# One transformer layer on one core: another written order for the MLP's up projection (transposes between products, early pairs begin with product 3) and two steps of the down projection split ahead

## The chip, the core and the metric

The kernel runs on one core of a Trainium2 chip. The core's engines have queues of their own and run at the same time: TensorE (PE: matmuls and transposes into PSUM banks, with PEld its weight loads), VectorE (DVE), ScalarE (ACT), GpSimd (POOL) and SyncE (SP, here a queue that issues DMAs). They wait for each other by semaphores. The metric is the device time of one execution in microseconds. The kernel before takes 1562.1 us (median of three runs, 1558.93 to 1566.71).

## What is computed

One layer of a hybrid encoder over 1024 tokens of width 1024 (plus 16 learned tokens): a combined input projection, neighbourhood attention, a gated linear recurrence in two directions, a gated mix with its output projection, and an MLP. The change lies in the MLP alone, the last third of the time:

```
D_MODEL = 1024
D_FF = 4 * D_MODEL
...
m = rms_norm(h, norm_mlp[l])
h = h + jnp.square(jax.nn.relu(m @ w_up[l])) @ w_down[l]
...
h = rms_norm(h, norm_final)
return h[:, N_META:]
```

All of it is float32. `m @ w_up` is a product of 1024 x 1024 with 1024 x 4096, and its squared positive part goes through `w_down` (4096 x 1024).

## The kernel before

**Float32 by three products.** A factor is split into a high half (`hi`, ACT casts it to `fp32r`) and a low half (`lo`, DVE subtracts the high half from the source). A product is then hi·hi + hi·lo + lo·hi. For a weight block `weights()` does this: ACT writes `wh` (L988), DVE writes `wl` (L989).

**Seven products for eight.** The 32 column blocks of `w_up` are taken as 16 *pairs* of 128-column blocks. For each pair the 2 x 2 block product is computed with seven block products instead of eight (a Winograd scheme). `pair_sums` makes the sums s1 to s4 of the weight blocks a11, a12, a21, a22 with four DVE operations (L682 to L685); the activations have sums of their own (t1 to t4). A block product is a `chain` of 12 matmuls of 128 x 512: four slices of the inner dimension, three matmuls each (L691, L692, L693). The seven are:

- product 1 (a11 x b11) and product 2 (a12 x b21, added on top) in a bank `pa`; ACT copies p1 out between the two (L1051), and the result is block u11.
- product 3 (s4 x b22) in a bank `pc`; ACT copies p3 out (L1061).
- product 6 (s2 x t2) in a bank `pb`; DVE makes u1 = pb + p1 (L1066).
- product 5 (s1 x t1) on top of `pc`; DVE adds pc to u1 (L1070), ACT applies relu and square.
- product 7 (s3 x t3) on top of `pb`; DVE makes u3 = pb + p1 (L1081), POOL subtracts p3 (L1082) and writes a block out (`block_out`, L1075).
- `finish_u3`: DVE adds pc (L1087), ACT relu and square, POOL two more blocks.
- product 4 (a22 x t4) on top of `pb`; DVE u2 = pb + p1 (L1096), ACT relu and square, POOL the last block.

Since a chain on top of a bank changes it, it has to wait until whoever read the bank's earlier content is done: product 7 waits for L1066, product 4 for L1081, product 5 for the copy p3, product 2 for the copy p1.

**Where the activations' variants come from.** The activations of half the layer (t1, b22, t3, t2, t4, each of four 128-row parts) must be transposed: 20 blocks. `to_variant` does one: four PE transposes into a bank `a` (L940), then ACT casts the bank to the high half (L942) and DVE makes the low half (L943). There are four such banks.

**The order.** From L1101 on the kernel stands in a `manual_schedule` for all five queues: each engine runs its instructions as the Python code issues them. Products 1 and 2 of the first three pairs (`EARLY = 3`) don't need the transposed blocks; they are computed ahead, while the 20 blocks are transposed between them in groups. Then the main loop runs over the pairs, with finish_u3 and product 4 of pair m - 1 inside the round of pair m, and with `next_weights`, which splits the weights of pair m + 1, spread between the products. An early pair has five chains in its round, a later one (a *steady* pair) seven. `load_pair` issues the 1 MB weight load of a pair two rounds ahead.

**The down projection** goes over 56 steps of two 128-row slices. Step 0 has its operands split (`step0`, four casts and four subtractions) in place of next weights in the last pair's round, and its 24 matmuls (L1178) run at once after the last product. The pools of the up projection are then closed; every later step is fetched (`fetch`, DMAs on SP), split (`prepare`, ACT L96 and DVE L97) and multiplied (L1169).

Of the kernel before, what the change touches and what calls it, by code (L numbers as in the profile page):

```python
# [18 lines left out]
P = 128  # L19
# [29 lines left out]
def layer(ctx: ExitStack, tc: tile.TileContext, x, meta, w_in, w_na, w_hg, w_o, w_up, w_dn,  # L49
# [636 lines left out]

    def chain(ps, lhs, rhs, first):

        for k in range(4):
            c = slice(k * P, (k + 1) * P)  # L690
            pe.matmul(ps, lhs[0][:, c], rhs[0][:, k], start=first and k == 0, stop=False, skip_group_check=True)  # L691
            pe.matmul(ps, lhs[0][:, c], rhs[1][:, k], start=False, stop=False, skip_group_check=True)  # L692
            pe.matmul(ps, lhs[1][:, c], rhs[0][:, k], start=False, stop=k == 3, skip_group_check=True)  # L693
# [278 lines left out]
    for v in ("t1", "t3", "t4"):  # L972
        nV[v] = [nvp.tile([P, 4, TH], F32R, name=f"n{v}{q}") for q in range(2)]
    psum_pools(pa=2, a=4)
    upa = ups.enter_context(tc.tile_pool(name="upa", bufs=1, reuse_waits="tile"))
# [36 lines left out]
    def load_pair(m):  # L1012
        t = rawp.tile([P, KC, 2 * P], F32, tag="raw", name="raw", bufs=2)
        if m < NP:
            sp.dma_start(t, w_up[:, 2 * m * P:(2 * m + 2) * P].rearrange("(k p) c -> p k c", p=P))
            pairs[m].raw = t
        else:

            t = t.rearrange("p k c -> p (k c)")
            sp.dma_start(t[:, :D].rearrange("p (q t) -> p q t", q=2), usp[0][0])  # L1020
            sp.dma_start(t[:, D:D + TH], w_dn[:P, :TH])
            sp.dma_start(t[:, D + TH:], w_dn[P:2 * P, :TH])
            step0_raw.append(t)

    step0_raw, step0 = [], []

# [19 lines left out]

    def product_1(q, w):
        q.p1, q.u11 = a_tile(upa, "p1", bufs=EARLY), a_tile(upa, "u11", bufs=EARLY)
        q.pa = up_bank("pa")
        chain(q.pa, w, nV["b11"], True)  # L1050
        act.copy(q.p1, q.pa)  # L1051

    def product_2(q, w):
        chain(q.pa, w, nV["b21"], False)
        relu2(q.u11, q.pa)
        (act if q.early or q.last else sp).dma_start(usp[0][q.m][:, 0], q.u11)
# [49 lines left out]
    with tc.manual_schedule(engines={e.engine for e in (pe, act, dve, pool, sp)}):  # L1106

        rs7 = row_scale(7)

        def transposes(n0, n1):  # L1110
            for n in range(n0, n1):
# [12 lines left out]
        transposes(9, 14)  # L1124
        product_2(pairs[1], first_w[1][1])
        transposes(14, 20)
        rows_.close()
# [102 lines left out]
    def fetch(ps_, m):  # L1230
        u = two("ur", bufs=3)
        sp.dma_start(u, usp[ps_][m])
        if ps_ == 0:
            load_w1(m)
            if m == 4:
                load_w1(0)
            if m >= NP - 3:
# [208 lines left out]
```

## Time and profile before

| | |
|---|---|
| median of three runs | 1562.1 us (1566.71, 1562.10, 1558.93) |
| the profiled execution's own time | 1566.63 us |
| its span, first to last instruction | 1564.9 us |
| mean granted clock of PE | 0.995 |
| transposes and first products, window | 912.80 to 943.95 us |
| rounds of pairs 0 to 2 | 943.95 to 994.30 us |
| rounds of pairs 3 to 15, and step 0 | 994.30 to 1250.85 us |
| turn to the down projection | 1250.85 to 1258.20 us |

A row of the timeline reads: start (us from the span's start), length, engine, line, operation, what is written and what is read, tile sizes, and in brackets how long the engine had been idle and which instruction ended that. Matmuls overlap, so the time from one start to the next says what one costs, not its length. A wait's row names the instruction that waits and the one it waits for.

### The profile page before, as it was taken

What the parts mean: (1) busy time and instruction counts of PE and PEld (TensorE: products, weight loads), DVE (VectorE), ACT (ScalarE), POOL (GpSimd) and SP (SyncE); (2) the same over time, 40 slices, a digit from 0 to 9 for tenths busy, and PEclk for the clock granted to TensorE, in tenths of its full rate; (3) what the DMA queues carried; (4) which work ended last, traced back from release to release, by engine and by line L of the source; (5) the groups of instructions that cost most, each with busy time, mean ns of one, the idle gap of its engine ahead of it and who ended that gap; (6) DMA issues with size and microseconds to landing.
All of it is one profiled execution on the core that took longest, in us unless ns stands there. A gap on an engine that the chain in (4) does not pass through costs nothing.

```text
span 1564.9 us, 23484 instructions
## 1 busy us (share of the span) xinstructions
PE 1506.5 (96%) x9188; PEld 1255.0 (80%) x9188; DVE 1027.7 (66%) x1588; ACT 655.2 (42%) x1172; POOL 405.4 (26%) x367
## 2 busy tenths in 40 slices
PE   6999999999999999999999988999999999999998
PEld 5788888878888877888888876788888778887886
DVE  6666666655886786666484456677777444879676
ACT  6131313125665575334132144455444543434444
POOL 5313131314404400101000212343434200237132
PEclk9999999999999999999999999999999999999999
DMA  5111011113122226436655123444444576562324
GB/s 179 42 28 55 28 56 28 55 35 121 66 80 92 95 86 217 142 115 207 222 168 202 41 95 101 141 148 148 157 151 161 186 248 234 198 234 100 108 81 148
DMA packets 142335, 195.61 MB, mean 125 GB/s; under 512 B 8064, under 2 KB 90112, under 8 KB 142224
## 3 DMA queue, kind: packets, MB, share of 16 engines
q1 hardware_dynamic: 133424, 172.61, 33.7%
q10 hardware_dynamic: 6624, 14.16, 2.3%
q0 software_dynamic: 2176, 7.34, 1.2%
q8 instruction: 72, 1.18, 0.3%
q14 instruction: 39, 0.32, 0.1%
HBM read 139.55 MB, written 54.53 MB: 124 GB/s over the span
## 4 chain that ended last, share of the span: by engine, by line
PE 84%; DVE 7%; ACT 3%; issue 3%; DMA 2%; POOL 1%; SPq 0%; ACTq 0%; POOLq 0%; DVEq 0%
PE mm L135 11%; PE mm L136 10%; PE mm L137 10%; PE mm L1169 4%; PE pa L1169 4%; PE pb L691 4%; PE pc L1169 4%; PE pb L692 4%; PE pb L693 4%; PE pb L1169 4%; PE pc L691 3%; PE pc L693 3%; PE pc L692 3%; PE pa L691 2%; PE pa L693 2%
## 5 line engine op out<-in xcount | busy, mean ns | idle before, releaser
L135 PE MATMUL mm<-aT,hi 128*128 128x512 f32 (+2 forms) x640 | 229.6, 359 | 2.7 <-DVE QX L563 1.5
L137 PE MATMUL mm<-aT,lo 128*128 128x512 f32 (+2 forms) x640 | 227.2, 355 | 0.0
L136 PE MATMUL mm<-aT,hi 128*128 128x512 f32 (+2 forms) x640 | 226.0, 353 | 0.0
L97 DVE TENSOR_TENSOR dl<-ur,dh 128x1024 fp32r<-128x1024 f32 x55 | 77.3, 1406 | 90.0 <-ACT dh L96 89.9
L135 PEld LDWEIGHTS mm<-aT,hi 128*128 128x128 f32 x640 | 121.3, 190 | 17.1 <-issue 1.7
L137 PEld LDWEIGHTS mm<-aT,lo 128*128 128x128 f32 x640 | 121.3, 189 | 13.2
L136 PEld LDWEIGHTS mm<-aT,hi 128*128 128x128 f32 x640 | 121.3, 190 | 12.4
L96 ACT CAST dh<-ur 128x1024 fp32r<-128x1024 f32 x55 | 57.9, 1053 | 164.4 <-issue 78.1
L125 ACT CAST hi<-raw 128x1024 fp32r<-128x1024 f32 x36 | 37.8, 1050 | 106.6 <-PE mm L136 75.5
L993 ACT ACTIVATE uv<-uv 128x512 f32<-128x512 f32 x48 | 30.4, 632 | 119.0 <-DVE uv L1096 66.4
L989 DVE TENSOR_TENSOR wl<-sx,wh 128x512 fp32r<-128x512 f32 x70 | 48.2, 696 | 41.6 <-ACT wh L988 41.6
L1082 POOL TENSOR_TENSOR uv<-uv,p 128x512 f32<-128x512 f32 x16 | 25.8, 1611 | 155.3 <-ACT wh L988 106.3
L989 DVE TENSOR_TENSOR wl<-raw,wh 128x512 fp32r<-128x512 f32 x46 | 42.2, 918 | 29.2 <-ACT wh L988 29.2
L1258 POOL TENSOR_TENSOR w<-w,tt 128x512 f32<-128x512 f32 x16 | 23.3, 1457 | 135.6 <-DVE tt L1257 115.7
L399 POOL TENSOR_TENSOR Y<-X,TN 128x512 f32<-128x512 f32 x20 | 33.8, 1690 | 88.1 <-DVE X L396 88.1
L126 DVE TENSOR_TENSOR lo<-raw,hi 128x1024 fp32r<-128x1024 f32 x34 | 44.1, 1297 | 15.5 <-ACT hi L125 15.4
L691 PE MATMUL pb<-nt,wh 128*128 128x512 f32 x128 | 50.2, 392 | 2.4 <-DVE uv L1081 2.4
L618 DVE CUSTOM_DVE_ANT_0 pr<-nsc,NB 128x432 f32<-128x432 f32 (+1 forms) x64 | 35.1, 558 | 26.4 <-PE nsc L613 26.2
L1169 PE MATMUL mm<-dl,dh 128*128 128x512 f32 x126 | 50.1, 397 | 2.1 <-DVE dl L97 2.1
L691 PE MATMUL pa<-nT,wh 128*128 128x512 f32 x128 | 50.4, 394 | 1.5 <-DVE hres L897 0.9
L1169 PE MATMUL mm<-dh 128*128 128x512 f32 x126 | 49.0, 391 | 1.6 <-ACT dh L96 1.6
L135 PE MATMUL mm<-wh,mT 128*128 128x512 f32 x128 | 50.2, 392 | 0.0
(380 smaller groups left out, 4402.2 us busy)
## 6 DMA issues: line engine op xcount, KB each, us to landing
raw<-in_w_in SPq DMA_DIRECT2D x56, 512.0 KB, 4.0
ur<-usp SPq DMA_DIRECT2D x55, 512.0 KB, 3.5
raw<-in_w_up SPq DMA_DIRECT2D x16, 1024.0 KB, 6.7
usp<-us SPq DMA_DIRECT2D x60, 256.0 KB, 3.1
sg<-gsp SPq DMA_DIRECT2D x16, 512.0 KB, 3.7
w<-in_w_dn SPq DMA_DIRECT2D x16, 512.0 KB, 5.1
usp<-uv SPq DMA_DIRECT2D x30, 256.0 KB, 3.9
gsp<-gv ACTq DMA_DIRECT2D x24, 256.0 KB, 2.6
```

Source lines behind the costliest of these rows:

```text
L96: act.copy(hi, src)
L97: dve.tensor_tensor(lo, src, hi.bitcast(F32), op=ALU.subtract)
L125: act.copy(hi[:, :kc], raw[:, :kc])
L126: eng.tensor_tensor(lo[:, :kc], raw[:, :kc], hi[:, :kc].bitcast(F32), op=ALU.subtract)
L135: pe.matmul(ps, lh, rh, start=first, stop=False)
L136: pe.matmul(ps, lh, rl, start=False, stop=False)
L137: pe.matmul(ps, ll, rh, start=False, stop=last)
L691: pe.matmul(ps, lhs[0][:, c], rhs[0][:, k], start=first and k == 0, stop=False, skip_group_check=True)
L692: pe.matmul(ps, lhs[0][:, c], rhs[1][:, k], start=False, stop=False, skip_group_check=True)
L693: pe.matmul(ps, lhs[1][:, c], rhs[0][:, k], start=False, stop=k == 3, skip_group_check=True)
L989: dve.tensor_tensor(v(lo), src, v(hi).bitcast(F32), op=ALU.subtract)
L1169: pe.matmul(ps, a[n == 2][:, q, j * P:(j + 1) * P], b[n == 1][:, q], start=first and n == 0, stop=last and n == 2, skip_group_check=True)
```

## The change

Three parts; the work done is the same.

1. *Transposes one by one.* `chain` takes a hook that is called before each of its four inner slices, and products 1 and 2 of pairs 0 and 1 use it to place one transposed block there. The 20 blocks, which stood in four groups, stand in 17.
2. *Order of the pairs.* The round of an early pair begins with product 3, ahead of finish_u3 and product 4 of the pair before and of the next pair's sums; product 6 follows, and the weight splits stand behind products 6, 5 and 7. In a steady pair the products keep their order; the splits of a11 and s4 now stand behind product 3, of a12 and s2 behind product 2, of s1 behind product 5, of s3 and a22 behind product 7.
3. *Two steps split inside.* Both step 0 and step 1 of the down projection are loaded by `load_pair`, their eight operands are split in the last pair's round, and 48 matmuls run before the pools are closed. `fetch` and `prepare` begin with step 2; a small load (`load_w1`) moves with them.

```
-    def chain(ps, lhs, rhs, first):
+    def chain(ps, lhs, rhs, first, between=lambda k: None):
         for k in range(4):
+            between(k)
...
-    psum_pools(pa=2, a=4)
+    psum_pools(a=4, pa=2)
...
-            sp.dma_start(t[:, :D].rearrange("p (q t) -> p q t", q=2), usp[0][0])
-            sp.dma_start(t[:, D:D + TH], w_dn[:P, :TH])
-            sp.dma_start(t[:, D + TH:], w_dn[P:2 * P, :TH])
-            step0_raw.append(t)
+            n, t = m - NP, t.rearrange("p k c -> p (k c)")
+            sp.dma_start(t[:, :D].rearrange("p (q t) -> p q t", q=2), usp[0][n])
+            sp.dma_start(t[:, D:].rearrange("p (q t) -> p q t", q=2),
+                         w_dn[2 * n * P:(2 * n + 2) * P, :TH].rearrange("(k p) c -> p k c", p=P))
+            step_raw.append(t)
...
+    def next_step():
+        n = len(step)
+        step.append(weights(step_raw[n // 4][:, n % 4 * TH:(n % 4 + 1) * TH]))
...
         if m + 1 == NP:
-            n = len(step0)
-            if n < 4:
-                step0.append(weights(step0_raw[0][:, n * TH:(n + 1) * TH]))
+            for v in vs:
+                next_step()
             return
...
-        product_1(pairs[0], first_w[0][0])
-        transposes(0, 4)
+        product_1(pairs[0], first_w[0][0], lambda k: transposes(1))
+        transposes(1)
         scale_row(7, rs7)
-        product_2(pairs[0], first_w[0][1])
-        transposes(4, 6)
+        product_2(pairs[0], first_w[0][1], lambda k: transposes(1))
         nB.append(row_sums(3))
-        transposes(6, 9)
-        product_1(pairs[1], first_w[1][0])
+        transposes(1)
+        product_1(pairs[1], first_w[1][0], lambda k: transposes(1))
+        transposes(1)
         first_weights(2)
-        transposes(9, 14)
-        product_2(pairs[1], first_w[1][1])
-        transposes(14, 20)
+        product_2(pairs[1], first_w[1][1], lambda k: transposes(1))
+        transposes(1)
...
-        psum_pools(pa=2, pb=2, pc=2)
+        psum_pools(pc=2, pb=2, pa=2)
...
-            if m + 2 <= NP:
+            if m + 2 < NP + 2:
                 load_pair(m + 2)
-            if not q.early:
-                product_1(q, q.W["a11"])
+            (product_3 if q.early else product_1)(q)
             if m:
                 finish_u3(pairs[m - 1])
             if m + 1 < NP:
                 pair_sums(pairs[m + 1])
             if m:
                 product_4(pairs[m - 1])
-            next_weights(m, "a11", "s4")
-            product_3(q)
-            next_weights(m, "a12")
-            if not q.early:
-                product_2(q, q.W["a12"])
-            next_weights(m, "s2")
-            product_6(q)
+            if q.early:
+                product_6(q)
+                next_weights(m, "a11", "s4", "a12", "s2")
+            else:
+                product_3(q)
+                next_weights(m, "a11", "s4")
+                product_2(q)
+                next_weights(m, "a12", "s2")
+                product_6(q)
+            product_5(q)
             next_weights(m, "s1")
-            product_5(q)
-            next_weights(m, "s3")
             product_7(q)
-            next_weights(m, "a22")
+            next_weights(m, "s3", "a22")
         finish_u3(pairs[-1])
         product_4(pairs[-1])
+        next_step()
...
-    for q in range(2):
-        for j in range(4):
-            for n in range(3):
-                pe.matmul(bk0[q][j], step0[q][n == 2][:, j * P:(j + 1) * P], step0[2 + q][n == 1],
-                          start=n == 0, stop=False, skip_group_check=True)
+    for i in (0, 4):
+        for q in range(2):
+            for j in range(4):
+                for n in range(3):
+                    pe.matmul(bk0[q][j], step[i + q][n == 2][:, j * P:(j + 1) * P], step[i + 2 + q][n == 1],
+                              start=i == 0 and n == 0, stop=False, skip_group_check=True)
...
-        us = {n: fetch(*steps[n]) for n in (1, 2)}
-        ready = prepare(*steps[1], us.pop(1))
+        us = {n: fetch(*steps[n]) for n in (2, 3)}
+        ready = prepare(*steps[2], us.pop(2))
...
-            if n == 0:
+            if n < 2:
                 continue
```

How the instructions move, at three places. Line numbers behind the changed `chain` are higher by one in the changed kernel, and by four to six further on.

PE, the end of product 1 of pair 0, before (`pt` is a transpose bank, `hres` and `t` are the activations' sums, `nT` the activations of product 1, `wh` and `wl` the weight's halves):

```order
L691 MATMUL pa<-nT_8818,wh 128x512
L692 MATMUL pa<-nT_8819,wh 128x512
L693 MATMUL pa<-nT_8818,wl 128x512
L940 MATMUL pt<-ident,hres_8493 128x128 x4
L940 MATMUL pt<-ident,hres_8494 128x128 x8
L940 MATMUL pt<-ident,t_8998 128x128 x4
L691 MATMUL pa<-nT_8818,wh 128x512
```

PE, product 1 of pair 0 from its start, of the changed kernel:

```order
L941 MATMUL pt<-ident,hres_8493 128x128 x4
L692 MATMUL pa<-nT_8818,wh 128x512
L693 MATMUL pa<-nT_8819,wh 128x512
L694 MATMUL pa<-nT_8818,wl 128x512
L941 MATMUL pt<-ident,hres_8494 128x128 x4
L692 MATMUL pa<-nT_8818,wh 128x512
L693 MATMUL pa<-nT_8819,wh 128x512
L694 MATMUL pa<-nT_8818,wl 128x512
L941 MATMUL pt<-ident,hres_8494 128x128 x4
```

Four blocks in a row have become one block after every three matmuls.

ACT, from product 5 of pair 0 to product 3 of pair 1, before (the `uv` rows are relu and square; `wh<-sx` is the cast of a sum's weight; `p<-pc` the copy p3):

```order
L993 ACTIVATE uv<-uv 128x512
L994 ACTIVATE uv<-uv 128x512
L988 CAST wh<-sx 128x512
L988 CAST wh<-raw 128x512
L993 ACTIVATE uv<-uv 128x512
L994 ACTIVATE uv<-uv 128x512
L993 ACTIVATE uv<-uv 128x512
L994 ACTIVATE uv<-uv 128x512
L988 CAST wh<-sx 128x512
L1061 COPY p_9616<-pc 128x512
L988 CAST wh<-sx 128x512 x2
```

ACT, the same stretch of the changed kernel:

```order
L994 ACTIVATE uv<-uv 128x512
L995 ACTIVATE uv<-uv 128x512
L989 CAST wh<-sx 128x512 x2
L989 CAST wh<-raw 128x512
L1065 COPY p_9576<-pc 128x512
L994 ACTIVATE uv<-uv 128x512
L995 ACTIVATE uv<-uv 128x512
L994 ACTIVATE uv<-uv 128x512
L995 ACTIVATE uv<-uv 128x512
L989 CAST wh<-sx 128x512 x2
```

The copy of pair 1's product 3 stood behind two relu-and-square groups and behind the cast of a sum for pair 2; now it stands ahead of all three.

ACT, around the last DMA of the up projection, before (`dh` is a high half of the down projection; `ur`, `b`, `w` are its fetched operands):

```order
L994 ACTIVATE uv<-uv 128x512
L1098 DMA usp_15_8528<-uv 128x512
L96 CAST dh<-ur 128x1024
L96 CAST dh<-b_1_11970 128x512
L96 CAST dh<-w_1_11972 128x512
```

ACT, the same place of the changed kernel:

```order
L995 ACTIVATE uv<-uv 128x512
L1102 DMA usp_15_8528<-uv 128x512
L989 CAST wh<-raw 128x512
L96 CAST dh<-ur 128x1024
L96 CAST dh<-b_2_12012 128x512
L96 CAST dh<-w_2_12014 128x512
```

The first operands that are fetched and split in the down projection's own way are those of step 2 (`b_2`), no longer those of step 1 (`b_1`); the last of the eight splits done in the up projection's way stands ahead of them.

More of the change, by code (lines that the diff above doesn't have):

```diff
@@ L1017, in load_pair @@
         else:
-            t = t.rearrange("p k c -> p (k c)")
-            sp.dma_start(t[:, :D].rearrange("p (q t) -> p q t", q=2), usp[0][0])
-            sp.dma_start(t[:, D:D + TH], w_dn[:P, :TH])
-            sp.dma_start(t[:, D + TH:], w_dn[P:2 * P, :TH])
-            step0_raw.append(t)
-    step0_raw, step0 = [], []
+            n, t = m - NP, t.rearrange("p k c -> p (k c)")
[3 more added lines that the diff above has]
+            step_raw.append(t)
+    step_raw, step = [], []
+    def next_step():
+        n = len(step)
+        step.append(weights(step_raw[n // 4][:, n % 4 * TH:(n % 4 + 1) * TH]))
     def pair_sums(q):
@@ L1045, in next_weights, with product_1, product_2 @@
                 q.W[v] = weights(q.A[v])
-    def product_1(q, w):
+    def product_1(q, w=None, between=lambda k: None):
         q.p1, q.u11 = a_tile(upa, "p1", bufs=EARLY), a_tile(upa, "u11", bufs=EARLY)
         q.pa = up_bank("pa")
-        chain(q.pa, w, nV["b11"], True)
+        chain(q.pa, w or q.W["a11"], nV["b11"], True, between)
         act.copy(q.p1, q.pa)
-    def product_2(q, w):
-        chain(q.pa, w, nV["b21"], False)
+    def product_2(q, w=None, between=lambda k: None):
+        chain(q.pa, w or q.W["a12"], nV["b21"], False, between)
         relu2(q.u11, q.pa)
@@ L1108, in layer, with transposes @@
         rs7 = row_scale(7)
-        def transposes(n0, n1):
-            for n in range(n0, n1):
+        count = [0]
+        def transposes(n):
+            for n in range(count[0], count[0] + n):
                 v = ("t1", "b22", "t3", "t2", "t4")[n % 5]
                 to_variant("a", nB[n // 5][v], nV[v], n // 5)
-        product_1(pairs[0], first_w[0][0])
-        transposes(0, 4)
+                count[0] += 1
+        product_1(pairs[0], first_w[0][0], lambda k: transposes(1))
+        transposes(1)
         scale_row(7, rs7)
-        product_2(pairs[0], first_w[0][1])
-        transposes(4, 6)
+        product_2(pairs[0], first_w[0][1], lambda k: transposes(1))
         nB.append(row_sums(3))
-        transposes(6, 9)
-        product_1(pairs[1], first_w[1][0])
+        transposes(1)
+        product_1(pairs[1], first_w[1][0], lambda k: transposes(1))
+        transposes(1)
         first_weights(2)
-        transposes(9, 14)
-        product_2(pairs[1], first_w[1][1])
-        transposes(14, 20)
+        product_2(pairs[1], first_w[1][1], lambda k: transposes(1))
+        transposes(1)
         rows_.close()
@@ L1234, in fetch @@
             load_w1(m)
-            if m == 4:
-                load_w1(0)
+            if m in (4, 5):
+                load_w1(m - 4)
             if m >= NP - 3:
```

## The prediction

> **What bounds the kernel now.** First the busy shares of the whole span, then the stages around the change, then what TensorE (PE) waits for there.
>
> ```profile
> PE 1506.5 (96%) x9188; PEld 1255.0 (80%) x9188; DVE 1027.7 (66%) x1588; ACT 655.2 (42%) x1172; POOL 405.4 (26%) x367
> ```
>
> PE is busy 96% of the span. Both kernels issue the same matmuls and transposes, so time can only go where PE stands still. The windows cut the up projection into transposes, early pairs (0 to 2) and steady pairs (3 to 15). Columns: window, length, busy time of PE, weight loads, DVE, ACT and POOL, granted clock, DMA share, GB/s.
>
> ```profile
> 912.80:943.95 31.15, 26.39 (x152) 22.00 (x153) 19.80 (x31) 17.91 (x33) 3.78 (x4) 1.00 0.31 103
> 943.95:994.30 50.35, 40.65 (x167) 31.79 (x167) 33.37 (x42) 20.91 (x37) 14.60 (x10) 0.97 0.40 131
> 994.30:1250.85 256.55, 256.55 (x1132) 211.99 (x1130) 174.90 (x210) 128.25 (x225) 97.98 (x69) 1.00 0.47 155
> ```
>
> The steady pairs have nothing to win: PE is busy 256.55 of 256.55 us, 0.2266 us a matmul, so a chain of 12 takes 2.72. The other two lose 4.8 and 9.7 us. The waits of PE between 905 and 1260 us (instruction, releaser, total, times, longest) name these losses, and at the turn to the down projection (L1169) 2.0 more:
>
> ```profile
> PE pc L691 <- ACT p L1061: 7.3, 3, 2.6
> PE pt L940 <- DVE nt L943: 4.0, 3, 1.4
> PE pb L691 <- DVE uv L1081: 2.4, 2, 1.2
> PE mm L1169 <- ACT dh L96: 1.6, 1, 1.6
> PE pa L691 <- DVE hres L897: 0.9, 1, 0.9
> PE pa L691 <- ACT p L1051: 0.7, 1, 0.7
> PE mm L1169 <- DVE dl L97: 0.4, 1, 0.4
> ```
>
> **Transposes.** Before, four groups of 4 or 5 blocks (16 or 20 transposes) fill the four transpose banks, and PE waits for a bank.
>
> ```profile
> 915.69 1.47 PE L940 MATMUL pt<-ident,hres 128*128 128x128 f32 x12
> 917.00 0.60 PE L940 MATMUL pt<-ident,t 128*128 128x128 f32 x4
> 917.35 0.48 PE L691 MATMUL pa<-nT,wh 128*128 128x512 f32 x1
> ...
> 920.17 1.91 PE L940 MATMUL pt<-ident,hres 128*128 128x128 f32 x16
> 923.40 0.66 PE L940 MATMUL pt<-ident,t 128*128 128x128 f32 x4 [1.31 <-DVE nt L943]
> ```
>
> ```profile
> 916.99 0.69 DVE L943 TENSOR_TENSOR nt<-pt,nt 128x512 fp32r<-128x512 f32 x1 [4.30 <-ACT nt L942]
> 917.60 0.68 DVE L943 TENSOR_TENSOR nT<-pt,nT 128x512 fp32r<-128x512 f32 x1
> ```
>
> Twelve transposes start within 917.00 - 915.69 = 1.31 us, 0.109 each. Sixteen should take 1.75, but 923.40 - 920.17 = 3.23: 1.48 lost, three times, 4.4 in all; a shorter stall inside the last groups brings it to 4.7. DVE empties a bank each 0.60 us (917.60 - 916.99). Now one block comes with every three matmuls: PE makes one per 4 x 0.109 + 3 x 0.2266 = 1.12 us, so DVE keeps up and all 4.7 go. The price is that 4 groups become 17. A group costs a switch: from 917.35 to 920.17 the chain took 2.82 where 12 x 0.2266 is 2.72, so 0.10, or 0.085 by the matmul starts alone. Thirteen more cost 1.1. The 0.9 on hres and the 0.7 on the copy of product 1 stay. Net **-3.6**. Bounds: -4.7 with free switches; -0.7 if each costs 0.31, a pause as long as the transposes' whole start-up (the 0.35 of the x4 row, 917.00 to 917.35, less one start).
>
> **Early pairs.** Read from one product 3 to the next:
>
> ```profile
> 952.13 0.50 PE L691 MATMUL pc<-nt,wh 128*128 128x512 f32 x1 [2.53 <-ACT p L1061]
> ...
> 955.20 0.69 DVE L1070 TENSOR_TENSOR uv<-uv,pc 128x512 f32<-128x512 f32 x1 [0.68 <-PE pc L693]
> ...
> 957.76 0.69 DVE L989 TENSOR_TENSOR wl<-sx,wh 128x512 fp32r<-128x512 f32 x1 [1.87 <-ACT wh L988]
> 958.37 0.68 DVE L1081 TENSOR_TENSOR uv<-pb,p 128x512 f32<-128x512 f32 x1
> ...
> 959.11 0.50 PE L691 MATMUL pb<-nt,wh 128*128 128x512 f32 x1 [1.22 <-DVE uv L1081]
> 959.20 1.60 POOL L1082 TENSOR_TENSOR uv<-uv,p 128x512 f32<-128x512 f32 x1 [31.53 <-DVE uv L1081]
> ...
> 959.44 0.40 PE L692 MATMUL pb<-nt,wh 128*128 128x512 f32 x1
> ...
> 960.83 0.69 DVE L1087 TENSOR_TENSOR uv<-uv,pc 128x512 f32<-128x512 f32 x1 [1.18 <-POOL uv L1082]
> ...
> 966.65 0.68 DVE L1096 TENSOR_TENSOR uv<-pb,p 128x512 f32<-128x512 f32 x1
> ...
> 969.19 2.02 DVE L989 TENSOR_TENSOR wl<-sx,wh 128x512 fp32r<-128x512 f32 x2 [1.86 <-ACT wh L988]
> ...
> 969.70 0.50 PE L691 MATMUL pc<-nt,wh 128*128 128x512 f32 x1 [2.12 <-ACT p L1061]
> ```
>
> A pair takes 969.70 - 952.13 = 17.57 us for five chains, 5 x 2.72 = 13.6. Two stalls: product 4 waits for the u3 addition, which stands on DVE behind a weight's low half (L989 at 957.76); and the chain after product 3 waits for the copy p3, which stands on ACT behind casts that wait for DVE's sums. The change puts product 3 of the next pair ahead of product 4, and p3 ahead of sums and casts. So both waits go: 7.3 + 2.4 = 9.7, and five restarts at 0.1 (959.11 to 959.44, 0.33 instead of 0.23), 10.2.
>
> What is late next is DVE's own round. Per early pair it issues 14 operations: four sums, five low halves (s4, s2, s1, s3, a22), three u additions with PSUM, two more additions with pc; 0.61 each (957.76 to 958.37), 8.4 us. Three of the sums are longer beside POOL:
>
> ```profile
> 949.66 0.68 DVE L684 TENSOR_TENSOR sx<-raw 128x512 f32<-128x512 f32 x1
> ...
> 961.44 1.17 DVE L682 TENSOR_TENSOR sx<-raw 128x512 f32<-128x512 f32 x1
> ...
> 962.93 1.55 POOL L1075 TENSOR_TENSOR us<-uv 128x512 f32<-128x512 f32 x1 [0.87 <-ACT uv L994]
> ...
> 963.25 1.78 DVE L684 TENSOR_TENSOR sx<-raw 128x512 f32<-128x512 f32 x1
> ...
> 964.95 1.78 DVE L685 TENSOR_TENSOR sx<-raw,sx 128x512 f32<-128x512 f32 x1
> ```
>
> L684 takes 0.68 alone and 1.78 while POOL writes a block, L685 likewise, and L682 1.17: 1.1 + 1.1 + 0.5, about 2.8 more, 11.2. Then the pauses no order removes: from the u1 addition through ACT to the low half of s1, 957.76 - 955.20 - 0.6 = 1.96; POOL's subtraction before the last u3 addition, 960.83 - 958.37 less three operations of 0.6 now queued there, about 0.6; from u2 through ACT to the next low half, 969.19 - 966.65 - 0.6 = 1.9 less one addition that now stands in it, 1.3. The round is 11.2 + 1.96 + 0.6 + 1.3 = 15.1 us against PE's 13.6: DVE becomes the bound by 1.5 a pair. Three rounds lie between product 3 of pair 0 and product 1 of pair 3, 4.5; following each instruction's producers at these durations gives new waits of 0.7, 0.6, 2.0 and 1.0, together 4.3, on the u3 or u1 addition before products 4 and 7. Net 10.2 - 4.3 = **-5.9**. Bounds: -10.2 with no new wait; -0.6 if all four sums take 1.78 (round 16.8, 3 x 3.2 lost).
>
> [...] The trace shows L684 longer by 1.1, less than the 1.55 of the POOL row beside it; were three sums longer by the full 1.55, the round would be 16.9 and the early pairs would gain next to nothing, which is rival (a) below.
>
> **Steady pairs.** PE's order is unchanged, but casts and low halves move: a12's low half now stands ahead of s2's, and so of the u1 addition that product 7 waits for.
>
> ```profile
> 1219.68 0.68 DVE L1066 TENSOR_TENSOR uv<-pb,p 128x512 f32<-128x512 f32 x1
> ...
> 1220.71 0.39 PE L691 MATMUL pb<-nt,wh 128*128 128x512 f32 x1
> ```
>
> Its result is seen 0.73 us after its start (958.37 to 959.11 above), at 1220.41; product 7 starts at 1220.71: 0.30 to spare in every steady pair. ACT's work ahead of it is the same set in another order, and a12's low half delays it by under 0.1, so I take **0**. If the cover goes, each 0.1 us beyond it costs 13 x 0.1 = 1.3. Bounds 0 and the delay of one whole operation: 0.6 - 0.3 over 13 pairs, +3.9; a gain is excluded, since PE has no idle time there.
>
> **The turn.** Step 1 of the down projection waited for tiles that step 0's last matmul freed, then for ACT (1.6) and DVE (0.4), with two restarts 2.2. Now step 1 is split before the up projection ends and its 24 matmuls, 24 x 0.2266 = 5.4 us, cover the 1.6 us of casts. Left is the low half of the next weights, whose memory PE's last product still frees: 0.4 before, and I keep 0.3 with its restart. The four extra weight splits on ACT and DVE fall in the last pair, which has no sums to make, so they are hidden; loads of step 4 still get two steps of 5.4. Net **-1.9**; bounds -2.2 and, if the extra splits cost 4 x 0.6 on the path, +0.2.
>
> **Clock.** Two windows of the profiled execution were granted half clock:
>
> ```profile
> 984.91:988.32 3.41, 0.80 (x4) 0.48 (x3) 1.58 (x2) 3.38 (x7) 1.26 (x1) 1.00 0.97 366
> 988.32:991.73 3.41, 3.41 (x9) 2.67 (x8) 2.83 (x5) 0.95 (x2) 0.00 (x0) 0.50 0.22 83
> ...
> 1251.15:1254.56 3.41, 1.57 (x6) 0.99 (x7) 2.60 (x5) 3.41 (x6) 0.54 (x1) 1.00 0.79 280
> 1254.56:1257.97 3.41, 3.41 (x10) 2.64 (x9) 2.29 (x3) 0.52 (x2) 0.00 (x0) 0.50 0.83 231
> ```
>
> Each followed a window in which PE was busy only 0.80 or 1.57 of 3.41 us, that is, a wait the change removes, and cost half of 3.41, 1.7. The profiled execution took 1566.6 us (span 1564.9; the 1.7 around it stays), near the slowest of the three runs (1558.9, 1562.1, 1566.7), so I read it as one that met both, and the median as one that met half: -3.4 against the profile, **-1.7** against the median. [...]
>
> **Sum.** -3.6 - 5.9 - 1.9 = -11.4, with the clock -14.8 on the profiled 1566.6 = 1551.8, and -13.1 on the median 1562.1 = **1549.0**.
>
> **Rivals.** (a) *DVE takes the early gain*: all sums meet POOL, early pairs give -0.6. For: L684 and L685 are 1.78 wherever POOL writes. Against: L683 stays short. 1562.1 - 3.6 - 0.6 - 1.9 - 1.7 = 1554.3 to 1556 without the clock: chance 0.13. (b) *Half clock stays*, because a new wait of 2.0 or another stall triggers it: 1562.1 - 11.4 = 1550.7, up to 1552.4 if one is added: 0.2. (c) *Switches cost 0.31*: -0.7 instead of -3.6, 1552: 0.08. (d) *Slower*: the u1 addition in the steady pairs comes late. From 0.3 us on PE waits 13 times; the gain of 13.1 is gone when each pair loses 1.0 (1.3 late), and the kernel is slower by 0.5% (7.8 us) from 1.6 a pair, say 1570. For: only 0.30 to spare. Against: the operations ahead of it are the same in number but one. Chance 0.04. (e) *The change does not do what it says*: waits return under other names (a bank not yet free, p3 still late), time within 4 us of before, 1560: 0.07. Forecast 0.48.
>
> **Range and chances.** About 0.5%, 7.8 us, is what a measurement of this kernel can tell from no change; the line lies at 1554.3. The forecast's own spread is 1543 (two thirds of the new DVE waits absent, 2.9, switches free, 1.1, all of the clock, another 1.7) to 1553 (the new DVE waits doubled); (b) and (c) lie inside, and (a) reaches 1556. The range 1543 to 1557 leaves out (d), (e) and a little on the low side. Faster: forecast, (b), (c) and a third of (a), 0.80; slower: (d), 0.04; the rest, 0.16, within.
>
> **What would show it.** No wait of a transpose on DVE's L944; 17 transpose groups, each first matmul after one about 0.31; no wait of pc on the copy p3; early waits only on u1 or u3 additions, 4 to 5 us in all; steady pairs still 19.03 us apart; the down projection with one wait of about 0.3; and no half clock after 985 us. I am wrong if the steady window shows PE waits, if DVE's round in the early pairs is nearer 17 than 15, or if the switches cost more than 0.1.

## The result and the profile after

The changed kernel takes **1554.0 us** (median of seven runs, 1553.04 to 1557.13); the kernel before, in seven runs, 1564.04. The ratio is 0.994, 95% interval 0.9923 to 0.9957: 9.4 us faster (10.0 by the two medians), a little more than half a per cent. Forecast were 1549.0 and a gain of 13.1. One execution of a later kernel, of 2794.7 us at a mean granted clock of 0.822, is left out of the times below. The profiled execution of the changed kernel has a span of 1553.7 us, 11.2 below the 1564.9 of before.

First the windows of the changed kernel, cut at the same places of the program as before: the transposes and the first products, the rounds of pairs 0 to 2, the rounds of pairs 3 to 15 with steps 0 and 1, and the turn (columns as in the prediction).

```profile
912.65:939.20 26.55, 25.84 (x152) 21.62 (x153) 19.53 (x30) 18.30 (x33) 3.79 (x4) 1.00 0.36 120
939.20:980.55 41.35, 39.06 (x169) 31.28 (x169) 33.15 (x40) 19.52 (x35) 15.65 (x10) 1.00 0.47 151
980.55:1248.90 268.35, 264.11 (x1153) 215.07 (x1153) 189.74 (x220) 135.10 (x237) 104.70 (x70) 1.00 0.48 158
1248.90:1254.80 5.90, 5.74 (x25) 4.43 (x25) 3.63 (x5) 0.05 (x1) 0.00 (x0) 1.00 0.87 266
```

The first two windows have shrunk from 31.15 to 26.55 and from 50.35 to 41.35 us, and no window here was granted half clock. But the third, in which PE was busy all the time before, now has 268.35 - 264.11 = 4.2 us of idle time: three waits of 2.5, 1.3 and 0.5 us in the rows below. A pause of 0.2 us is not in it, since a matmul's row, 0.39 us or more, is longer than the 0.23 us between two starts; such pauses are read from the starts. The waits of PE in the changed kernel between 905 and 1260 us:

```profile
PE pb L692 <- DVE uv L1085: 3.8, 2, 2.5
PE pb L692 <- DVE uv L1070: 2.1, 2, 1.3
PE pt L941 <- DVE hres L898: 0.8, 1, 0.8
PE pa L692 <- ACT p L1055: 0.7, 1, 0.7
PE pb L1185 <- DVE uv L1100: 0.5, 1, 0.5
PE mm L1175 <- DVE dl L97: 0.2, 1, 0.2
```

The waits for a transpose bank, for the copy p3 and for ACT's casts at the turn are gone. In their place PE waits for DVE's additions to u1 (L1070, before product 7) and u2 (L1100, before the down projection takes the bank), and longer than before for the one to u3 (L1085, before product 4; 2.4 us before, 3.8 now).

Counted from one matmul's start to the next, in the two profiles:

| | before | after | change | forecast |
|---|---|---|---|---|
| transposes with the four products around them | 24.65 | 20.02 | -4.6 | -3.6 |
| stalls from product 3 of pair 0 to product 7 of pair 3 | 10.5 | 6.9 | -3.6 | -5.9 |
| rounds of pairs 4 to 15, up to step 0's first matmul | 228.5 | 230.4 | +1.9 | 0 |
| stalls at the turn | 2.7 | 1.2 | -1.5 | -1.9 |
| half clock in this part | 3.4 | 0 | -3.4 | -3.4 (-1.7 of the median) |

The sum is -11.2, as much as the spans differ by. A stall is counted here from the start of the last matmul ahead of it, less the 0.23 us of that matmul; the restart behind it, about 0.1, is not in it. A round of the steady pairs takes 19.04 us before and 19.23 after as a mean, 19.1 and 19.3 by turns; the last one, which has no sums to make, loses nothing.

### The profile page after: what moved, and what is told of

Same layout as the page of the kernel before. It is cut to its first block, busy times and chain, and to the rows that moved or that the text cites. A ratio compares the mean times of both kernels' runs of the same rounds, so it can differ in the third digit from the quotient of the medians.

```text
span 1553.7 us, 23462 instructions
## 1 busy us (share of the span) xinstructions
PE 1504.5 (97%) x9188; PEld 1252.5 (81%) x9188; DVE 1040.5 (67%) x1589; ACT 655.1 (42%) x1173; POOL 412.4 (27%) x367
## 5 line engine op out<-in xcount | busy, mean ns | idle before, releaser
L990 DVE TENSOR_TENSOR wl<-raw,wh 128x512 fp32r<-128x512 f32 x50 | 55.5, 1115 | 45.2 <-ACT wh L989 45.2
L990 DVE TENSOR_TENSOR wl<-sx,wh 128x512 fp32r<-128x512 f32 x70 | 48.0, 696 | 31.8 <-ACT wh L989 31.7
L1086 POOL TENSOR_TENSOR uv<-uv,p 128x512 f32<-128x512 f32 x16 | 25.9, 1619 | 141.9 <-ACT wh L989 105.5
L92 POOL TENSOR_SCALAR rtm<-ssq 128x1 f32<-128x1 f32 (+1 forms) x17 | 6.6, 391 | 173.3 <-ACT junk L920 159.2
```

The costliest lines, as they stand in the source:

```text
L990: dve.tensor_tensor(v(lo), src, v(hi).bitcast(F32), op=ALU.subtract)
```

## The experiments

**Each part alone.** The first three kernels are the kernel before with one part of the change. The transposes:

```
-        product_1(pairs[0], first_w[0][0])
-        transposes(0, 4)
+        product_1(pairs[0], first_w[0][0], lambda k: transposes(1))
+        transposes(1)
...
```

> The kernel before with only the transposes placed one by one. If a switch between a transposed block and matmuls costs 0.085 us more than the border between two blocks, the stretch from the first product to product 1 of pair 2 takes 21.1 us and the kernel gains 3.6 (1560.4). If a block's border costs the same whatever follows it, the stretch takes 20.0 us as in the changed kernel and the kernel gains 4.6 (1559.4). Waits in the early pairs and at the turn as in the kernel before.

Measured: 1558.2 us, ratio 0.9968 (0.9956 to 0.9979), 5.0 us gained. From the first product to product 1 of pair 2 it took 20.00 us: the second of the two expectations. A row of the waits was not foreseen:

```profile
PE pc L692 <- ACT u L994: 0.7, 1, 0.7
```

It is neither in the profile before nor in the one after. This kernel has the new order of the bank pools ahead of the early products and the old one behind them; the next kernel has the two the other way round, and the same 0.7. With both old or both new it is absent, so the change's two lines on `psum_pools` belong together. It costs less than 0.7: in this kernel the wait for the copy p3 that follows it is 1.0 shorter (6.3 in all instead of 7.3), and in the next one the first stall on the u1 addition, 0.3, is gone.

The early order alone:

```
-            if not q.early:
-                product_1(q, q.W["a11"])
+            product_3(q) if q.early else product_1(q, q.W["a11"])
...
+            if q.early:
+                product_6(q)
+                next_weights(m, "a11", "s4", "a12", "s2")
+                product_5(q)
+                next_weights(m, "s1")
+                product_7(q)
+                next_weights(m, "s3", "a22")
+            else:
...
```

> The kernel before with only the early pairs' order changed; in the steady pairs the weight splits stay at their old places. The early waits should be those of the changed kernel (6.9 us of stalls instead of 10.5, on u3 and u1 additions): 3.6 gained, and up to 1.7 more where no half clock follows: 1558.7 to 1560.4. Theory: the steady pairs' loss of about 0.2 us a pair comes from the new places of their splits, so here they are 19.03 us apart. Rival: it comes from the early pairs' backlog; then they are 19.2 apart here too, and the time is 1561 to 1563.

Measured: 1558.3 us, ratio 0.9964 (0.995 to 0.9977), 5.6 gained, a little better than expected. The early waits are 3.8 on the u3 addition and 0.8 on the u1 addition, and steady pairs are 19.04 apart again: the early pairs' backlog doesn't reach pairs 4 to 15.

The two steps alone:

```
-            if m + 2 <= NP:
+            if m + 2 < NP + 2:
                 load_pair(m + 2)
...
+    for i in (0, 4):
+        for q in range(2):
...
-        us = {n: fetch(*steps[n]) for n in (1, 2)}
+        us = {n: fetch(*steps[n]) for n in (2, 3)}
```

> The kernel before with only the two steps of the down projection split ahead. The stall at the turn should fall from 2.7 us to about 1.2, and the half clock after it may go: 1560.8 to 1562.5. If the four more splits in the last pair cost anything, a wait shows in that pair's round and the gain is below 1 us.

Measured: 1560.1 us, ratio 0.9979 (0.9968 to 0.999), 3.3 gained, a little more than expected; at the turn only the wait for a low half is left (0.2). The four further splits cost nothing that the trace shows.

The three ratios leave 0.0032 + 0.0036 + 0.0021 = 0.0089 of the time, 13.9 us; the whole change brings 9.4. What all three lack is the new places of the splits in the steady pairs. The fourth kernel is the changed one without these:

```
             else:
+                next_weights(m, "a11", "s4")
                 product_3(q)
-                next_weights(m, "a11", "s4")
+                next_weights(m, "a12")
                 product_2(q)
-                next_weights(m, "a12", "s2")
+                next_weights(m, "s2")
                 product_6(q)
+                next_weights(m, "s1")
+                product_5(q)
+                next_weights(m, "s3")
+                product_7(q)
+                next_weights(m, "a22")
```

> The changed kernel with the steady pairs' weight splits at their old places (early pairs, transposes and the turn as changed). Theory: in the steady pairs the low half of a22 now runs beside POOL's subtraction for u3 and takes 1.78 instead of 0.68 us, which makes product 7 wait about 0.2 us in each of 13 pairs; with the old places it is 0.68 again, pairs are 19.03 apart and the kernel takes about 1551.4. Rival: the loss is POOL's or the DMAs' and has nothing to do with the splits; then 1554 as the changed kernel.

Measured: 1551.2 us, ratio 0.9918 (0.9901 to 0.9935), steady pairs 19.03 apart. So the new places in the steady pairs cost 2.8 us of the change's gain; in the traces it is 1.9 in the rounds and 0.5 at the turn. The two intervals overlap at their ends (the changed kernel's begins at 0.9923); the distance of the pairs in the two traces does not. The mechanism that was put down with it held only in part, as follows.

**Why the steady pairs lost.** In the changed kernel a22's low half (L990) meets POOL's subtraction for u3 (L1086), DVE and POOL rows of one steady pair:

```profile
1158.78 0.68 DVE L990 TENSOR_TENSOR wl<-sx,wh 128x512 fp32r<-128x512 f32 x1
1159.00 1.62 POOL L1086 TENSOR_TENSOR uv<-uv,p 128x512 f32<-128x512 f32 x1 [7.78 <-ACT wh L989]
1159.38 1.78 DVE L990 TENSOR_TENSOR wl<-raw,wh 128x512 fp32r<-128x512 f32 x1
...
1161.08 0.67 DVE L1091 TENSOR_TENSOR uv<-uv,pc 128x512 f32<-128x512 f32 x1
```

The low half takes 1.78 us instead of 0.68, and the next addition is late. With the splits at their old places (the fourth kernel) it starts ahead of POOL and takes 0.68:

```profile
1151.37 0.69 DVE L1074 TENSOR_TENSOR uv<-uv,pc 128x512 f32<-128x512 f32 x1
...
1153.92 0.69 DVE L990 TENSOR_TENSOR wl<-sx,wh 128x512 fp32r<-128x512 f32 x1 [1.87 <-ACT wh L989]
1154.53 0.68 DVE L1085 TENSOR_TENSOR uv<-pb,p 128x512 f32<-128x512 f32 x1
1155.13 0.68 DVE L990 TENSOR_TENSOR wl<-raw,wh 128x512 fp32r<-128x512 f32 x1
1155.35 1.61 POOL L1086 TENSOR_TENSOR uv<-uv,p 128x512 f32<-128x512 f32 x1 [8.15 <-ACT wh L989]
```

Two kernels were to show that this is the cause. One takes POOL out of the chain:

```
         act.copy(q.p3, q.pc)
+        pool.tensor_tensor(q.p3, q.p1, q.p3, op=ALU.subtract)
...
-        dve.tensor_tensor(q.u3, q.pb, q.p1, op=ALU.add)
-        pool.tensor_tensor(q.u3, q.u3, q.p3, op=ALU.subtract)
+        dve.tensor_tensor(q.u3, q.pb, q.p3, op=ALU.add)
```

> The changed kernel with POOL's subtraction for u3 taken out of the chain: POOL makes p1 - p3 right after product 3's copy, and DVE adds that to product 7 (same sum, in another order). The splits stay at the changed kernel's places. Theory: the steady pairs lose 0.2 us each because a22's low half runs beside that subtraction; without it there the low half takes 0.68 and pairs are 19.03 apart though the splits have not moved back: 1551 to 1552. Rival: the loss is only that a12's low half stands ahead of the u1 addition (0.1); then pairs stay over 19.1 apart and the time near 1554. Early waits: 6.9 to 4 if the subtraction meets nothing at its new place, unchanged if it lengthens the sums.

> The same kernel as in the run with p1 - p3 made ahead at the changed kernel's places, for a profile that can be read: pairs 19.03 apart by the theory of POOL beside a22's low half, over 19.1 apart if it is a12's low half ahead of the u1 addition. Time 1552 to 1553 as then.

Measured: 1552.6 us (ratio 0.9928, 0.9915 to 0.9941), and 1551.2 (0.992, 0.990 to 0.994) in the second group of runs, whose profile is the one read here: steady pairs 19.04 apart. The early waits, expected at 4 us or unchanged, are 6.3 counted from the starts (6.9 in the changed kernel). The low half of a22 takes 0.68 and the addition behind it follows at once:

```profile
1155.01 0.68 DVE L1086 TENSOR_TENSOR uv<-pb,p 128x512 f32<-128x512 f32 x1
1155.61 0.68 DVE L990 TENSOR_TENSOR wl<-sx,wh 128x512 fp32r<-128x512 f32 x1
1156.21 0.68 DVE L990 TENSOR_TENSOR wl<-raw,wh 128x512 fp32r<-128x512 f32 x1
1156.81 0.68 DVE L1091 TENSOR_TENSOR uv<-uv,pc 128x512 f32<-128x512 f32 x1
```

The other moves s3's split ahead of product 7 in the steady pairs, so that a22's low half starts ahead of POOL while all else stays changed:

```
-            next_weights(m, "s1")
+            next_weights(m, "s1", *(() if q.early else ("s3",)))
             product_7(q)
-            next_weights(m, "s3", "a22")
+            next_weights(m, *(("s3", "a22") if q.early else ("a22",)))
```

> The changed kernel with one split moved: in the steady pairs s3's weight is split ahead of product 7, as before the change; a11, s4, a12, s2, s1 and a22 stay where the change puts them. Theory: then a22's low half follows the u3 addition directly, starts 0.1 us ahead of POOL's subtraction and takes 0.68 us, not 1.78; the steady pairs are 19.05 apart and the time is 1551 to 1552. Rival: the steady loss comes from a12's low half ahead of the u1 addition; then pairs stay 19.2 apart and the time at 1554.

Measured: 1554.5 us, ratio 0.9937 (0.9919 to 0.9954), steady pairs 19.31 apart: **the theory fell**. The low half did take 0.68, as wanted, and the pairs were further apart than in the changed kernel. A loss, and a larger one, comes about without POOL beside a22's low half; that meeting is one way in which the loss arises, not its cause.

What fits all of them is the length of one stretch on DVE: from the pc addition to u1 (L1074, which waits for product 5) to the next pair's u1 addition (L1070, which product 7 waits for; lines of the changed kernel). Product 7 can start when product 5's last matmul is out; L1074 starts about 0.2 us behind that point, and L1070's result is seen 0.73 us after its start. In a pair of 19.03 us the stretch may therefore take 19.03 - 0.21 - 0.73 = 18.09 us. From the start times in the traces, ten pairs each, all stretches within 0.03 of each other, the distance of the pairs as a mean; the third column is the part of the stretch up to the pc addition to u3 (L1091):

| kernel | stretch, us | up to L1091 | rest | pairs apart, us |
|---|---|---|---|---|
| before | 17.80 | 5.63 | 12.17 | 19.04 |
| changed, steady splits as before | 17.80 | 5.63 | 12.17 | 19.03 |
| changed | 18.33 | 6.07 | 12.26 | 19.23 |
| changed, s3 ahead of product 7 | 18.50 | 6.24 | 12.26 | 19.31 |
| changed, p1 - p3 made ahead | 16.70 | 5.67 | 11.03 | 19.04 |

The two that are over 18.09 are the two that lose. Before, s1's low half stood on DVE between the u1 addition and the pc addition, where DVE has to wait for PE anyway; the change moves it behind the pc addition, into the stretch. There DVE now has three low halves ahead of L1091, where it had two. The u3 addition itself is no later, 3.17 us behind the pc addition in both, since it queues behind one low half in both, s3's before and s1's now. But behind it s3's low half now takes the place ahead of POOL's subtraction, which was a22's, and a22's starts only when POOL has: 0.44 (6.07 instead of 5.63). A12's low half adds 0.09 in the rest. With s3 ahead as well, the u3 addition queues behind two low halves, starts at 3.77, and L1091 is 0.61 late although a22's low half doesn't meet POOL.

The pairs of the changed kernel are 19.1 and 19.3 us apart by turns because a wait of product 7 and its restart, 0.16 and 0.13, hold PE back for one round, in which DVE catches up; in the next round product 7 loses only 0.08.

Two further kernels test this with one split each:

```
+            if not q.early:
+                next_weights(m, "s1")
             product_5(q)
-            next_weights(m, "s1")
+            if q.early:
+                next_weights(m, "s1")
             product_7(q)
```

> The changed kernel with only s1's split put back ahead of product 5 in the steady pairs. New theory: what counts is DVE's stretch from the pc addition to u1 (behind product 5) to the next u1 addition that product 7 waits for; up to 18.09 us product 7 never waits. It is 17.80 with the old places, 18.33 in the changed kernel, 18.50 with s3 ahead. With s1's low half back in DVE's idle time before the stretch, it should be about 17.9, pairs 19.04 apart and the time 1551 to 1552, although a22's low half still meets POOL. Rival (a22's low half beside POOL is by itself the cause): 19.2 apart and 1554.

```
-                product_2(q)
-                next_weights(m, "a12", "s2")
+                next_weights(m, "a12")
+                product_2(q)
+                next_weights(m, "s2")
```

> The changed kernel with only a12's split put back ahead of product 2 in the steady pairs. By the stretch: 18.33 - 0.08 = 18.25, still above 18.09, so pairs are 19.15 to 19.2 apart and the time is 1553 to 1554. If a12's low half were the cause of the loss, 19.04 and 1551.5.

Measured with s1 back: stretch 17.87, pairs 19.07 apart, 1551.2 us, ratio 0.9914 (0.9895 to 0.9932), though a22's low half still takes 1.78 beside POOL. Nothing stands ahead of the u3 addition there (it starts at 2.70), so that L1091 is at 5.61 in spite of the meeting. The 0.03 by which the pairs are further apart than worked out stays open. With a12 back: stretch 18.25, pairs 19.19 apart, as worked out; its time, 1551.7, ratio 0.9915 (0.9894 to 0.9936), is lower than expected and by itself would fit the rival. The interval reaches up to 0.9936 x 1563.4 = 1553.4, so the expected time isn't excluded; by time these two kernels can't be told apart, by the traces they can.

**The early pairs.** Two waits on the u3 addition are left there, 1.3 and 2.5 us. This is the second one in the changed kernel:

```profile
982.10 0.68 DVE L1074 TENSOR_TENSOR uv<-uv,pc 128x512 f32<-128x512 f32 x1
...
984.01 1.12 ACT L989 CAST wh<-sx 128x512 fp32r<-128x512 f32 x2
984.64 0.69 DVE L990 TENSOR_TENSOR wl<-sx,wh 128x512 fp32r<-128x512 f32 x1 [1.87 <-ACT wh L989]
...
985.25 0.68 DVE L1085 TENSOR_TENSOR uv<-pb,p 128x512 f32<-128x512 f32 x1
...
985.99 0.50 PE L692 MATMUL pb<-nt,wh 128*128 128x512 f32 x1 [2.50 <-DVE uv L1085]
```

DVE idles 1.87 us ahead of s1's low half, waiting for ACT, while the u3 addition behind it could run: product 7 ended at 980.6. So, with the steady splits at their old places:

```
                 product_5(q)
-                next_weights(m, "s1")
                 product_7(q)
-                next_weights(m, "s3", "a22")
+                next_weights(m, "s1", "s3", "a22")
```

> The changed kernel with the steady splits at their old places and, in the early pairs, product 7 issued ahead of the splits of s1, so that DVE makes the u3 addition as soon as product 7 ends and not behind s1's low half, which waits for ACT. Theory: product 4's two waits (1.3 and 2.5) are that queueing and nothing else; they go, and the kernel takes 1548 to 1549. Rival: DVE's round is simply too long, the wait moves to the next product on the round (the u1 addition, or a weight's low half), and the time stays at 1551.

Measured: 1547.0 us, ratio 0.9885 (0.9872 to 0.9898), the fastest kernel of the study. The waits of PE from 905 to 1260 us in this kernel, and DVE in the same place:

```profile
PE pt L941 <- DVE hres L898: 0.8, 1, 0.8
PE pc L692 <- ACT p L1065: 0.8, 1, 0.8
PE pa L692 <- ACT p L1055: 0.7, 1, 0.7
PE pb L692 <- DVE uv L1070: 0.5, 1, 0.5
PE mm L1180 <- DVE dl L97: 0.2, 1, 0.2
```

```profile
979.25 0.67 DVE L1074 TENSOR_TENSOR uv<-uv,pc 128x512 f32<-128x512 f32 x1
979.85 0.68 DVE L1085 TENSOR_TENSOR uv<-pb,p 128x512 f32<-128x512 f32 x1
981.80 2.40 DVE L990 TENSOR_TENSOR wl<-sx,wh 128x512 fp32r<-128x512 f32 x2 [1.27 <-ACT wh L989]
```

The addition runs at once, inside what was idle time, and both waits are gone; of the early pairs' 4.7 us of waits in the fourth kernel 1.3 are left. It was queueing, not a round too long to fit. A half-clock window, which the fourth kernel's profile has at the 2.5 us wait and this one's doesn't, is not what the 4.2 us between the two medians are made of: from product 3 of pair 0 to product 1 of pair 4, counted from the starts, the fourth kernel loses 7.6 us with that window, the changed kernel 7.7 without one, and this kernel 2.4.

POOL's subtraction made ahead was also tried on the fourth kernel and on this one:

> The changed kernel with the steady splits at their old places (as in the run before this one) and p1 - p3 made ahead. The steady pairs have no wait left, so only the early pairs can gain: the round of DVE loses the wait on POOL and the 1.1 us beside it, up to 1.1 a round: 1548 to 1551.

> Both: steady splits at their old places, product 7 ahead of the splits of s1 in the early pairs, and p1 - p3 made ahead by POOL. If the early waits are queueing, nearly all of the 5.6 us left there go and the kernel takes 1546 to 1548; if DVE's round is the bound, it is no better than the kernel without one of the two.

Measured: 1550.2 us (0.9905, 0.9891 to 0.992) and 1547.5 (0.9892, 0.9879 to 0.9904), neither distinguishable from the kernel without it. The waits tell why: the fourth kernel's 4.7 us on the two additions became 5.7, one of them 3.3 long, and this kernel's 0.5 on the u1 addition became 2.3. The subtraction at its new place meets other operations of DVE: in the fourth kernel's variant POOL is busy from 942.20 to 943.68, and a single operation of DVE fills the whole microsecond from 943.00 to 944.00, where the operations of the changed kernel at this place take 0.68 or 0.69 with POOL idle.

## Why the forecast was right, and where its terms were off

The time lies inside the range, but two of the signs that the forecast named for being wrong came: PE waits in the steady window, and DVE's round in the early pairs is nearer 17 than 15 us. These two terms missed by 1.9 and 2.3 us, and by luck 1.0 of it came back from transposes that cost less than forecast. Of the 5.0 us between 1549.0 and 1554.0, 1.9 is that the median of the kernel before moved from 1562.1 to 1564.0.

**Transposes, -3.6 forecast, -4.6 measured.** The waits went as worked out. The price of 13 more switches, 1.1, was wrong: it was counted twice. In the changed kernel a block and its matmuls read:

```profile
913.88 0.60 PE L941 MATMUL pt<-ident,hres 128*128 128x128 f32 x4
914.23 0.48 PE L692 MATMUL pa<-nT,wh 128*128 128x512 f32 x1
914.55 0.40 PE L693 MATMUL pa<-nT,wh 128*128 128x512 f32 x1
...
915.01 0.60 PE L941 MATMUL pt<-ident,hres 128*128 128x128 f32 x4
```

A block takes 0.35 us up to the first matmul and the switch 0.10 more, 0.45 in all; in a group of twelve transposes a block took 0.44. The 0.109 per transpose, taken from a group, already held a pause at each block's border. Rival (c), dear switches, is refuted by the same rows.

**Early pairs, -5.9 forecast, -3.6 measured.** First a slip: the rows at 952.13 and 969.70 that the prediction reads as product 3 are product 5, the chain on top of `pc` that waits for the copy p3. The period, the stalls and their causes are as stated. The mechanism was right, and the new waits stand on the two additions that were named: 0.7, 0.6, 2.0 and 1.0 forecast, 1.5, 1.0, 2.7 and 1.4 measured from the starts, and one of 0.3. The mis-sized term is DVE's round of 15.1 us: from one u3 pc addition to the next it took 16.41 (954.15 to 970.56). In the last round (to 988.15) it took 17.59, since a11's and a12's low halves for pair 3, which the count of 14 operations leaves out, come on top. The prediction let only the sums be longer beside POOL, and these took 5.2 us, as forecast. What it left out are low halves beside POOL. The first case stands in a row that the prediction shows, two low halves of 2.02 at 969.19, and was counted as 1.2. In the changed kernel:

```profile
962.13 1.30 POOL L1079 TENSOR_TENSOR us<-uv,us 128x512 f32<-128x512 f32 x1 [2.62 <-ACT uv L995]
962.53 2.05 DVE L990 TENSOR_TENSOR wl<-sx,wh 128x512 fp32r<-128x512 f32 x2 [1.28 <-ACT wh L989]
964.50 0.67 DVE L1074 TENSOR_TENSOR uv<-uv,pc 128x512 f32<-128x512 f32 x1
```

That is 1.97 instead of 1.2, 0.8 a round. In the second case POOL's subtraction for u3 falls on a22's low half:

```profile
952.45 1.78 DVE L990 TENSOR_TENSOR wl<-raw,wh 128x512 fp32r<-128x512 f32 x1
954.15 0.68 DVE L1091 TENSOR_TENSOR uv<-uv,pc 128x512 f32<-128x512 f32 x1
```

Its 1.1 us more is not all lost, since L1091 would have had to wait for POOL in any case: from the u3 addition (951.25) to L1091 it is 2.90 where the forecast has 2.4, 0.5 a round. The two make up the 1.3 by which the round was longer. Rival (a), DVE taking the whole early gain, was the right direction and went less than half of the way, and not by the sums that it named. And the 1.96, one of "the pauses no order removes", could be filled by another order, as the kernel with product 7 first showed.

**Steady pairs, 0 forecast, +1.9 measured.** The step that failed is "ACT's work ahead of it is the same set in another order, and a12's low half delays it by under 0.1". It looked only at what stands directly ahead of the u1 addition (0.09 in the traces). The rest, 0.44, came round from the pair before: s1's low half stands in DVE's stretch, and a22's is pushed into POOL's subtraction. The bound given for this term, 0 to +3.9, held it. Rival (d) is this mechanism, at a tenth of the size that would have made the kernel slower: its margin of 0.30 us was right, and used up.

**The turn, -1.9 forecast, -1.5 measured.** One new wait was not named: the last of step 0's banks is the `pb` bank that the u2 addition of the last pair still reads.

```profile
1242.68 0.50 PE L1185 MATMUL pb<-wh 128*128 128x512 f32 x1 [0.46 <-DVE uv L1100]
```

It is not there when the steady splits stand at their old places.

**Clock.** Both half-clock windows that the profile before has in this part are gone, -3.4 as forecast. But a wait of 2.5 us is left, on the u3 addition, and of the six profiles that have it, five had half clock right around its end (983 to 986 us in the fourth kernel, 984 to 988 with a12 back); only the changed kernel's own profile had none. So the new wait that rival (b) names is there, and some executions of the changed kernel may well meet half clock behind it. It hardly costs anything at this place: from product 3 of pair 0 to product 1 of pair 4 the five lose 7.4 to 7.8 us with the window, the changed kernel 7.7 without. Where PE ran at half clock there, product 7 of pair 3 no longer waits 1.3 us for DVE's u1 addition: in the fourth kernel 0.9 us of waits on it are left in all, in the changed kernel 2.1. How often the kernel before meets its two windows, and so what the median gained by the clock, was not measured. Rival (b) is not needed for the miss: the steady pairs, the early pairs, the transposes and the turn make it up, with 1.9 + 2.3 - 1.0 + 0.4 = 3.6 us, against the 3.7 by which the gain fell short.

Rival (e) is out by the time. The waits for a transpose bank, for p3 and for ACT at the turn went away; the one of product 4 on the u3 addition did not, it grew.

## What to carry to other kernels

When instructions are moved on an engine that is not the bottleneck, add up its whole round between the two points where the bottleneck meets it, not only what stands directly ahead of the wait; the split of s1 put into idle time ahead of the round left the pairs 19.07 us apart, the same split inside it 19.23. Among operations that wait for different engines, issue first the one whose input is ready first: one line that let the u3 addition pass a low half brought more, 4.2 us, than the change's new order of the steady splits had cost, 2.8. Take the price of a switch from the same rows as the price of what it separates, or it is counted twice.

## What the runs showed of the hardware

In the rows read here, an operation of DVE with two inputs in SBUF took longer where POOL had started first, and ended about 0.55 us behind POOL's end. In the changed kernel the low half issued at 1159.38 ends at 1161.16, 0.54 us behind POOL's subtraction (1159.00 + 1.62 = 1160.62); in the fourth kernel, started 0.22 us ahead of POOL, it took 0.68. The prediction held the 1.1 us by which L684 is longer against the whole 1.55 of POOL's row; but L684 was issued 0.32 us after POOL had started (963.25 against 962.93), and it too ended 0.55 us behind POOL's end (965.03 against 964.48), so that its 1.78 is the 1.23 that POOL still took and 0.55.

Whether half clock followed a wait did not go by the wait's length alone. The same 2.5 us wait of PE was met by half clock in five profiles (983 to 986 us in the fourth kernel, for one) and not in that of the changed kernel; a wait of 3.25 us in the fourth kernel's variant with p1 - p3 made ahead (982.59 to 985.84) was not met by it either. The half-clock windows in this part of the kernel before are 3.41 us long. In the five profiles with half clock, PE was busy only 0.88 to 1.44 us of the 3.41 us ahead of it; in the kernel before, half clock also followed 3.41 us with 1.57 busy. But in the 3.41 us that end with the wait, PE was busy 0.91 us in the changed kernel (982.58 to 985.99) and 0.16 in the variant, and no half clock came. What decides it was not shown.
